# Softmax sums applied to the gate tile instead of p, and hi and lo of p accumulated in the same columns

## The chip, the core and the metric

The kernel runs on one core of a Trainium2 chip. The metric is device microseconds for one execution of the whole program, as a median of runs. Engines are named as in the profile: PE is TensorE's matmul, PEld its weight load, DVE is VectorE, ACT ScalarE, POOL GpSimd, and SP the engine that issues all the DMAs here.

## What is computed

One inference step of a streaming encoder layer, for 2048 new frames of one stream ("prompt") and 64 frames of a running one ("sample"), in float32:

```
h = h + W_out( concat[ attnA(xn) * silu(gA), hgrn2(xn) * silu(gB) ] ),  xn = RMSNorm(h)
...
s = jnp.einsum('bnqhd,bnkhd->bnhqk', q, k).astype(jnp.float32) * ATTN_SCALE + bias
s = jnp.where(valid[None, :, None], s, NEG_INF)
p = jax.nn.softmax(s, axis=-1).astype(v.dtype)
return jnp.einsum('bnhqk,bnkhd->bnqhd', p, v)
...
o_a = attn_fn(heads(aq), k, v).reshape(B, T, W_A) * jax.nn.silu(ag)
```

Group A is attention with 8 heads of 64: each chunk of 64 frames sees its own chunk and the 8 before it, with a learned bias. Group B is a gated linear recurrence with 4 heads of 128. The change is in group A alone: in the softmax, in p times v, and in the product with the gate silu(gA).

## The kernel before

Frames are taken in four stages (`SUPER`) of 512, 576, 512 and 512, the second of which also holds the 64 sample frames. In each stage TensorE multiplies 32 column blocks of W_in with xn (tiles `acc`), and the attention and the recurrence of the heads whose columns are there run between these multiplications. The last stage is followed by the output projection, also in `acc`. Float32 accuracy comes from splitting operands into a high and a low part (`xh` and `xl`, `w` as a pair, `q` and `ql`, v as [hi | lo] in 128 stationary columns, p as `ph[:, 0]` and `ph[:, 1]`) and adding up the products.

The order of instructions on every engine is fixed when the program is built. Generators describe the pieces of work; a planner (`Plan`, called `C`) keeps an estimated clock for each engine and lets a generator go on when its next piece looks ready (`yield "A", t` means: when the plan's ScalarE gets to time t). Tokens (`tk`) stand for buffers: `pr` (4 tiles of p), `ph` (2), `pv` (1 PSUM bank), `mixa` (2), `sga` (2, the gate), and so on. `C.mm(n)` charges TensorE 12 + n/2.37 ns for a matmul of n columns. Each engine works through its list in order, and a wait of the instruction at the head holds all behind it. SP's list holds the weight loads (`w<-wd`, L437) and every other transfer.

Attention works by pairs of heads, and in a pair by units of 256 queries and one head: (g0, h) with g0 = 0, 256 and h = 0, 1. There are 64 such units. In each:

- `softmax_rows` (L895), once for each 128 queries: scores in PSUM (`s`), bias added and the row's extreme taken by DVE (L911), then `softmax_exp` (L925): ScalarE's exponential with the row sum accumulated (L928), DVE's reciprocal of the sum (L931), and DVE's scaling of the up to 640 columns of p by it (L932).
- `p_group` transposes p through PSUM (`tr`, L253), and `split_p` writes hi (ScalarE, L940) and lo (DVE, L943) of the transposed p to `ph`.
- `attend` (L986) multiplies with v. One matmul (L1038) takes hi and lo of one key block side by side: a key block that both 128-query blocks see gives 2 x 256 = 512 moving columns; the two that only one sees give 2 x 128 = 256. PSUM tile `pv` is 128 partitions (64 of v's hi, 64 of v's lo) x 2 halves (p's hi, p's lo) x 256 queries.
- `finish_pv` (L975): ScalarE copies p_hi v_lo to `mixa` (L978), DVE adds p_hi v_hi and p_lo v_hi (L982).
- `mix_out` (L1081), for a pair's two heads together: POOL multiplies `mixa` with the gate `sga` (L1084), and SP stores it to DRAM (`mixd`, L1089). The output projection reads it back from there much later.

The sample frames go through `sample_a`, which has its own scores and p times v and uses `softmax_exp`, `finish_pv` and `mix_out`.

Of the kernel before, what the change touches and what calls it, by code (L numbers as in the profile page):

```python
# [8 lines left out]
F32 = mybir.dt.float32  # L9
F32R = mybir.dt.float32r  # L10
U32 = mybir.dt.uint32
AF = mybir.ActivationFunctionType
# [5 lines left out]
P = 128  # L18
D = 1024
KT = D // P  # L20
SEQ = 2048
DEC = 64
# [7 lines left out]
PRB = 4  # L30
VTB = 3
# [152 lines left out]
def hymba_step(  # L184
# [24 lines left out]
    act = nc.scalar  # L209
    dve = nc.vector  # L210
    pool = nc.gpsimd
    pe = nc.tensor
    sp = nc.sync
# [12 lines left out]
    def T(pool_, shape, dt, tag, **kw):  # L226
        uid[0] += 1
        return pool_.tile(list(shape), dt, tag=tag, name=f"{tag}_{uid[0]}", **kw)

    def psum(tag, shape=(P, 512), bufs=1):  # L230
        return T(ps, shape, F32, tag, bufs=bufs)
# [16 lines left out]
    def mm(out, w, x, n, slow=False, **kw):  # L248
        pe.matmul(out, w, x, **kw)  # L249
        C.mm(n, slow)  # L250

    def transpose(out, x, idn):
        pe.transpose(out, x, idn)  # L253
        C.now += 110.0

    tk = {k: Tok(C, n) for k, n in dict(acc=2, s_ps=1, tr=2, pv=1, g=1, pr=PRB, ph=2, sig=2, vT=VTB, mixa=2,
                                     w=WBUFS, raw=RAWB, xn=XNB, kv0=1, kv1=1, rec=1, sga=2, bias0=1, bias1=1, gf=1, gi=1, gg=1,
                                     ck=1, slot=4, x4=0, x5=0).items()}

# [632 lines left out]

        return d, dict(g=ev_g, q=ev_q, k=ev_k, v=ev_v_last if last else ev_v)

    def softmax_rows(d, h, qc, spans, bcol, nk, out):  # L895

        yield lambda: d.q_n[h] >= qc + P and d.k_n[h] >= qc + P and d.bias_at[h] is not None
        yield max(d.q_t[h], d.k_t[h], d.bias_at[h]) + 300.0
        yield from tk["s_ps"].get()
        yield from tk["pr"].get()  # L900
        sps = s_ps()
        for part in (d.q, ql):
            for i, (k0, kn) in enumerate(spans):
                mm(sps[:, i, :kn], part[:, h, qc : qc + P], d.kd[:, h, k0 : k0 + kn], kn,
                   start=part is d.q, stop=part is ql)
        t = C.pe()
        yield "D", t
        s = T(wk, [P, 640], F32, "pr", bufs=PRB)
        nm = T(wk, [P, 2], F32, "nm", bufs=4)
        ns, kn = len(spans), spans[0][1]  # L910
        dve.tensor_tensor_reduce(  # L911
            s[:, :nk].rearrange("p (a c) -> p a c", a=ns), sps[:, :ns, :kn],
            d.bias[:, h, bcol : bcol + nk].rearrange("p (a c) -> p a c", a=ns),
            1.0, 3e38, ALU.add, ALU.min, nm[:, 0:1])
        t = C.dve(nk + 80, t)
        tk["s_ps"].put(1, t)
        d.left[h] -= 1
        if d.left[h] == 0:
            if h and d.sb == len(SUPER) - 1 and d.p == NPAIR - 1:
                have.add("scores")  # L920
                tk["x4"].put()
            tk[f"bias{h}"].put()
        yield "A", t
        yield from softmax_exp(s, nm, nk, out, t)

    def softmax_exp(s, nm, nk, out, t):
        sm = T(wk, [P, 1], F32, "sm", bufs=4)
        act.activation(s[:, :nk], s[:, :nk], AF.Exp, bias=nm[:, 0:1], scale=-1.0, accum_out=sm)  # L928
        t = C.act(nk + 300, t)
        yield "D", t  # L930
        dve.reciprocal(sm, sm)  # L931
        dve.tensor_scalar(s[:, :nk], s[:, :nk], sm, None, ALU.mult)  # L932
        t = C.dve(0.55 * nk + 150, t)
        out.append((s, t))

    def vcols(v, t, h, rows):
        return (v[:rows, h, t] if v is room["v"] else v[:rows, t, 2 * h : 2 * h + 2, :]).rearrange("p s d -> p (s d)")
# [34 lines left out]
        tk["tr"].put(1, t)  # L972
        done.append((ph, t))

    def finish_pv(h, pv, mix, qn, t):  # L975

        hs, ls = own[h], own[1 - h]
        act.copy(mix[hs, :qn], pv[ls, 0, :qn])  # L978
        t = C.act(qn, t)
        yield "D", t  # L980
        for i in range(2):
            dve.tensor_add(mix[hs, :qn], mix[hs, :qn], pv[hs, i, :qn])  # L982
            t = C.dve(qn, t)
        return t

    def attend(d, g0, h, prs, mixes, before, mine):  # L986

        t0 = SUPER[d.sb][0]
        b0 = (t0 + g0) // P
        base = t0 // P - 4  # L990
        yield lambda: len(prs[0]) and len(prs[1])
        yield max(prs[0][0][1], prs[1][0][1]) + 300.0

        def piece(kt, b):
            pr = prs[b][0][0]
            nk = min(5, b0 + b + 1) * P
            first = b0 + b + 1 - nk // P
            return (pr, (kt - first) * P, b * P)

        items = [(kt - base, P, [piece(kt, 0), piece(kt, 1)]) for kt in range(max(0, b0 - 3), b0 + 1)]  # L1000
        if b0 - 4 >= 0:
            items.append((b0 - 4 - base, P, [piece(b0 - 4, 0)]))
        items.append((b0 + 1 - base, P, [piece(b0 + 1, 1)]))
        groups, cur, used = [], [], 0
        for it in items:
            w = P * len(it[2])
            if used + w > 512:
                groups.append(cur)
                cur, used = [], 0
            cur.append((it, used))  # L1010
            used += w
        groups.append(cur)
        dones = [[] for _ in groups]
        yield lambda: before is None or before["spawned"]
        for i, (g, dn) in enumerate(zip(groups, dones)):
            C.spawn(p_group(g, dn, 2 if i == len(groups) - 1 else 0, turn["given"]), 1)
            turn["given"] += 1
        mine["spawned"] = True
        yield lambda: before is None or before["pv"]
        yield from tk["pv"].get()  # L1020
        mine["pv"] = True
        if h == 0:
            yield from tk["mixa"].get()
            mixes[g0] = T(wk, [P, 256], F32, "mixa", bufs=2)
        mix = mixes[g0]
        yield lambda: d.v_n[h] >= g0 + 256
        yield d.v_t[h]
        pv = psum("pv").rearrange("p (s q) -> p s q", s=2)
        k = 0
        for g, dn in zip(groups, dones):  # L1030
            yield lambda: len(dn)
            ph, t = dn[0]
            yield t + 200.0
            for it, off in g:
                t_, kr, qs = it
                w = P * len(qs)
                q0 = qs[0][2]
                mm(pv[:, :, q0 : q0 + w], vcols(d.v, t_, h, kr), ph[:kr, :, off : off + w], 2 * w,  # L1038
                   start=(k == 0), stop=(k == len(items) - 1))
                k += 1  # L1040
            tk["ph"].put(1, C.pe())
        t = C.pe()
        yield "A", t
        t = yield from finish_pv(h, pv, mix, 256, t)
        tk["pv"].put(1, t)
        mine["end"] = True
        if h:
            yield from mix_out(d, mix, g0, 256, t, g0 + 256 == SUPER[d.sb][1])

    last_mark = [None]  # L1050

    def attention(d):

        sb, p = d.sb, d.p
        t0, n = SUPER[sb][:2]
        npr = min(n, WIN)
        units = [(g0, h) for h in range(2) for g0 in range(0, npr, 256)]
        d.left = [len(units) + (1 if npr < n else 0)] * 2
        allprs = []
        for g0, h in units:  # L1060
            prs = [[], []]
            for b in range(2):
                blk = (t0 + g0) // P + b
                nk = min(5, blk + 1) * P
                qc = g0 + b * P
                k0 = 512 + qc + P - nk
                spans = [(k0, 320), (k0 + 320, 320)] if nk == 640 else [(k0, nk)]
                C.spawn(softmax_rows(d, h, qc, spans, 640 - nk, nk, prs[b]), 1)
            allprs.append(prs)
        marks = [dict(spawned=False, pv=False, end=False) for _ in units]  # L1070
        mixes = {}
        for i, ((g0, h), prs) in enumerate(zip(units, allprs)):
            C.spawn(attend(d, g0, h, prs, mixes, marks[i - 1] if i else last_mark[0], marks[i]), 1)
        last_mark[0] = marks[-1]
        if npr < n:
            yield from sample_a(d, npr, marks)
        for h in range(2):
            yield lambda: all(m["end"] for m, u in zip(marks, units) if u[1] <= h)
            tk[f"kv{h}"].put(1, C.pe())

    def mix_out(d, mix, g0, n, t, last):  # L1081
        yield lambda: d.sg_n >= g0 + n
        yield "P", t
        pool.tensor_mul(mix[:, :n], mix[:, :n], d.sg[:, g0 : g0 + n])  # L1084
        t = C.pool(n + 50, t)
        if last:
            tk["sga"].put()
        yield t
        sp.dma_start(mixd[d.sb][d.p, :, g0 : g0 + n], mix[:, :n])  # L1089
        tk["mixa"].put()  # L1090
        done_a[d.sb] = done_a.get(d.sb, 0) + n
# [32 lines left out]
    def sample_a(d, c0, marks):  # L1124
# [74 lines left out]
        t = C.pe()  # L1199
        yield "A", t  # L1200
        for h in range(2):
            t = yield from finish_pv(h, pv[:, h], mix, DEC, t)
        tk["pv"].put(1, t)
        tk["raw"].put(2)
        C.spawn(mix_out(d, mix, c0, DEC, t, True), 1)
# [953 lines left out]
```

## Time and profile before

| what | value |
|---|---|
| median of 3 runs | 1257.12 us (1254.45 to 1257.91) |
| profiled execution | 1256.82 us |
| its span (first to last instruction) | 1254.6 us |
| mean granted TensorE clock | 0.996 of full speed |
| ACT L928, exponentials of the softmax | 132, 100.3 us |
| DVE L943, lo of the transposed p | 176, 101.4 us |
| DMA queue of SP | 67.4% of 16 engines' time, 286.58 MB |

The profile is of one execution. A row of groups reads: line, engine, operation, out<-in, shape, count | busy us, mean ns of one | idle time of the engine just before it, and what ended it. A row of the timeline reads: start, length of the run of like instructions (both in us), engine, line, operation, shape, count. A row of stretches reads: the stretch, its length, the busy time and count of PE, PEld, DVE, ACT, POOL, then the granted TensorE clock, the DMA engines' busy share and GB/s. A row of waits reads: who waited for whom, us in total, times, longest. A row of DMA issues: out<-in, queue, count, KB each, median us from issue to landing.

### The profile page before, as it was taken

How to read it: one execution, taken by the hardware profiler on the slowest of the kernel's cores; microseconds unless marked ns; L12 is line 12 of the kernel's file. 1: busy time of each engine (PE TensorE's matmuls, PEld its weight loads, DVE VectorE, ACT ScalarE, POOL GpSimd, SP SyncE). 2: the span in 40 equal slices, each digit the busy share in tenths (PEclk: the TensorE clock that was granted, in tenths of full speed). 3: DMA queues.
4: the chain of work that ended last, by engine and by line, in shares of the span. 5: the costliest groups of instructions: out<-in, count | busy, mean ns of one | idle time of the engine just before them, and what ended most of it. 6: DMA issues, size and time to landing. Idle time of an engine off the chain costs nothing. (4 is left out here: it accounts for less than half of the span.)

```text
span 1254.6 us, 21417 instructions
## 1 busy us (share of the span) xinstructions
PE 1240.9 (99%) x7550; PEld 1093.7 (87%) x7550; DVE 894.6 (71%) x1887; ACT 684.7 (55%) x1533; POOL 415.2 (33%) x700
## 2 busy tenths in 40 slices
PE   8999999999999999999999999999999999999997
PEld 8888888999999999998888888988888888888786
DVE  6687879766867678687486667785857476867775
ACT  5354546654656556574465556665655445643443
POOL 6666665111120110201233242134241103474543
PEclk9999999999999999999999999999999999999999
DMA  8987779656555476655777878677666665987431
GB/s 334 311 306 248 279 285 370 212 158 228 178 189 159 145 223 216 193 166 172 252 266 240 299 255 281 227 248 251 219 244 202 222 219 197 342 275 241 136 125 67
DMA packets 137956, 287.94 MB, mean 230 GB/s; under 512 B 35257, under 2 KB 79289, under 8 KB 120186
## 3 DMA queue, kind: packets, MB, share of 16 engines
q1 hardware_dynamic: 137560, 286.58, 67.4%
q8 instruction: 59, 0.97, 0.3%
q14 instruction: 47, 0.39, 0.1%
q10 hardware_dynamic: 290, 0.01, 0.0%
HBM read 195.31 MB, written 92.27 MB: 229 GB/s over the span
## 5 line engine op out<-in xcount | busy, mean ns | idle before, releaser
L249 PE MATMUL acc<-xh,w 128*128 128x512 f32 (+2 forms) x2752 | 566.4, 345 | 0.7 <-ACT xh L403 0.4
L249 PEld LDWEIGHTS acc<-xh,w 128*128 128x128 f32 x2752 | 439.8, 189 | 50.4 <-issue 0.6
L249 PE MATMUL acc<-xl,w 128*128 128x512 f32 (+2 forms) x1376 | 293.4, 345 | 0.3 <-DVE xl L407 0.3
L249 PEld LDWEIGHTS acc<-xl,w 128*128 128x128 f32 x1376 | 220.2, 189 | 25.1 <-DVE xl L407 0.5
L928 ACT ACTIVATE pr<-pr,nm 128x640 f32<-128x640 f32 (+4 forms) x132 | 100.3, 760 | 59.7 <-DVE nm L911 58.8
L940 ACT CAST ph<-tr 128x512 fp32r<-128x512 f32 (+3 forms) x176 | 87.9, 507 | 74.1 <-PE pv L249 47.8
L464 POOL TENSOR_TENSOR w<-wraw,w 128x256 fp32r<-128x256 f32 x120 | 106.6, 914 | 56.9 <-DVE w L459 40.4
L943 DVE TENSOR_TENSOR ph<-tr,ph 128x512 fp32r<-128x512 f32 (+3 forms) x176 | 101.4, 588 | 27.6 <-ACT ph L940 26.8
L911 DVE CUSTOM_DVE_ANT_0 pr<-s,bias 128x640 f32<-128x640 f32 (+4 forms) x128 | 94.2, 736 | 34.8 <-PE s L249 34.1
L249 PE MATMUL pv<-ph,v 128*128 128x256 f32 (+2 forms) x344 | 97.8, 370 | 0.0
L253 PE MATMUL tr<-ident,pr 128*128 128x128 f32 x580 | 89.0, 273 | 1.4 <-DVE sig L634 0.6
L500 POOL TENSOR_TENSOR xn<-wraw,xn 128x256 fp32r<-128x256 f32 x48 | 39.4, 822 | 142.2 <-ACT xn L497 136.4
L982 DVE TENSOR_TENSOR mixa<-mixa,pv 64x256 f32<-64x256 f32 (+1 forms) x144 | 56.8, 395 | 36.0 <-ACT mixa L978 32.7
L1084 POOL TENSOR_TENSOR mixa<-mixa,sga 128x256 f32<-128x256 f32 (+1 forms) x36 | 29.1, 808 | 158.8 <-DVE mixa L982 146.3
L932 DVE TENSOR_SCALAR pr<-pr,sm 128x640 f32<-128x640 f32 (+4 forms) x132 | 76.9, 583 | 4.7
L253 PEld LDWEIGHTS tr<-ident,pr 128*128 128x128 f32 x580 | 69.9, 140 | 10.8 <-DVE sig L634 1.0
L1521 POOL TENSOR_TENSOR k<-ob 128x512 f32<-128x512 f32 (+2 forms) x20 | 18.2, 911 | 180.7 <-ACT ob L1512 161.9
L564 ACT ACTIVATE sig<-acc 128x512 f32<-128x512 f32 (+2 forms) x64 | 32.0, 499 | 64.8 <-PE acc L249 61.7
L249 PEld LDWEIGHTS pv<-ph,v 128*128 128x128 f32 (+1 forms) x344 | 58.4, 189 | 7.1
L978 ACT COPY mixa<-pv 64x256 f32<-64x256 f32 (+1 forms) x72 | 25.1, 349 | 62.3 <-PE pv L249 58.7
L249 PE MATMUL s<-kd,q 128*128 128x320 f32 (+2 forms) x232 | 56.5, 314 | 0.0
L249 PE MATMUL s<-kd,ql 128*128 128x320 f32 (+2 forms) x232 | 55.7, 310 | 0.0
(324 smaller groups left out, 2140.2 us busy)
## 6 DMA issues: line engine op xcount, KB each, us to landing
w<-wd SPq DMA_DIRECT2D x96, 1024.0 KB, 5.6
wd<-w SPq DMA_DIRECT2D x32, 1024.0 KB, 7.7
wraw<-in_w_in_dram SPq DMA_DIRECT2D x30, 512.0 KB, 5.6
wod<-xn SPq DMA_DIRECT2D x28, 512.0 KB, 5.4
xn<-in_x_prompt_dram SPq DMA_DIRECT2D x23, 512.0 KB, 4.6
bias<-biasd SPq DMA_DIRECT2D x24, 320.0 KB, 5.8
carry<-kd SPq DMA_DIRECT2D x12, 512.0 KB, 3.7
carry<-v SPq DMA_DIRECT2D x12, 512.0 KB, 6.7
```

The lines of the kernel that those rows point to most:

```text
L249: pe.matmul(out, w, x, **kw)
L253: pe.transpose(out, x, idn)
L464: pool.tensor_sub(w[:, 1, k : k + 2], raw[:, k : k + 2], f32(w[:, 0, k : k + 2]))
L500: pool.tensor_sub(f32r(st[:, c.start + 512 : c.stop + 512]), src[:, c], st[:, c])
L564: act.activation(sig[:, :bn], acc, AF.Exp, scale=-1.0)
L911: dve.tensor_tensor_reduce(s[:, :nk].rearrange("p (a c) -> p a c", a=ns), sps[:, :ns, :kn], d.bias[:, h, bcol : bcol + nk].rearrange("p (a ...
L928: act.activation(s[:, :nk], s[:, :nk], AF.Exp, bias=nm[:, 0:1], scale=-1.0, accum_out=sm)
L932: dve.tensor_scalar(s[:, :nk], s[:, :nk], sm, None, ALU.mult)
L940: act.copy(ph[:krows, 0, :wid], pt[:krows, :wid])
L943: dve.tensor_sub(ph[:krows, 1, :wid], pt[:krows, :wid], f32(ph[:krows, 0, :wid]))
L982: dve.tensor_add(mix[hs, :qn], mix[hs, :qn], pv[hs, i, :qn])
L1084: pool.tensor_mul(mix[:, :n], mix[:, :n], d.sg[:, g0 : g0 + n])
```

## The change

Three things are changed in the attention of the prompt frames.

1. p is no longer scaled. `softmax_rows` takes the exponential itself and leaves the two row sums of a unit side by side in a tile `sums`; p goes on unnormalised to the transposes.
2. A new generator `weigh` takes the reciprocals of both sums at once, stores them to DRAM as two rows of 128 (`way`, 4 bytes at a time, since a query is a partition in `sums`), and when both heads of a query pair are there, loads them back into `rr`: head 0's 256 numbers into each of 64 partitions, head 1's into the other 64. `mix_out` multiplies the gate tile with `rr` on POOL, and then `mixa` with the gate as before. `rr` has one buffer, guarded by a token.
3. In `attend` hi and lo of p are two matmuls that accumulate in the same 256 columns of `pv`, instead of one that writes both halves beside each other. `finish_pv` then adds one part fewer. (p_lo v_lo is now part of the result too; before, it was computed and not read.)

The sample frames keep the old scaling and the old halves.

```diff
-    def softmax_rows(d, h, qc, spans, bcol, nk, out):
+    def softmax_rows(d, h, qc, spans, bcol, nk, out, sums):
...
-        yield from softmax_exp(s, nm, nk, out, t)
+        if "t" not in sums:
+            sums["t"] = T(wk, [P, 2], F32, "sums", bufs=3)
+        b = qc // P % 2
+        act.activation(s[:, :nk], s[:, :nk], AF.Exp, bias=nm[:, 0:1], scale=-1.0, accum_out=sums["t"][:, b : b + 1])
+        out.append((s, C.act(nk + 300, t)))
+
+    def weigh(d, g0, h, prs, sums, spread):
+
+        yield lambda: len(prs[0]) and len(prs[1])
+        yield "D", max(prs[0][0][1], prs[1][0][1])
+        dve.reciprocal(sums["t"], sums["t"])
+        yield C.dve(60)
+        uid[0] += 1
+        room = dr.tile([2, P], F32, tag=f"way{uid[0]}", name=f"way{uid[0]}")
+        sp.dma_start(room.rearrange("b q -> q b"), sums["t"])
+        t = C.dma(16)
+        spread[g0, h] = room
+        if h == 0:
+            return
+        yield from tk["rr"].get()
+        rr = spread[g0] = T(wk, [P, 256], F32, "rr", bufs=1)
+        yield t
+        for i in range(2):
+            sp.dma_start(rr[own[i]], spread[g0, i].rearrange("(o b) q -> o (b q)", o=1).broadcast_to([64, 256]))
+        sums["at"] = C.dma(32)
...
-        act.copy(mix[hs, :qn], pv[ls, 0, :qn])
+        act.copy(mix[hs, :qn], parts[0][ls])
...
-        for i in range(2):
-            dve.tensor_add(mix[hs, :qn], mix[hs, :qn], pv[hs, i, :qn])
+        for x in parts:
+            dve.tensor_add(mix[hs, :qn], mix[hs, :qn], x[hs])
...
-        pv = psum("pv").rearrange("p (s q) -> p s q", s=2)
+        pv = psum("pv")[:, :256]
...
-                mm(pv[:, :, q0 : q0 + w], vcols(d.v, t_, h, kr), ph[:kr, :, off : off + w], 2 * w,
-                   start=(k == 0), stop=(k == len(items) - 1))
-                k += 1
+                for part in range(2):
+                    mm(pv[:, q0 : q0 + w], vcols(d.v, t_, h, kr), ph[:kr, part, off : off + w], w,
+                       start=k == 0, stop=k == 2 * len(items) - 1)
+                    k += 1
...
+        if by:
+            yield lambda: "at" in by[1]
+            yield "P", by[1]["at"]
+            rr = by[0][g0]
+            pool.tensor_mul(d.sg[:, g0 : g0 + n], d.sg[:, g0 : g0 + n], rr[:, :n])
+            tk["rr"].put(1, C.pool(n + 50))
         yield "P", t
         pool.tensor_mul(mix[:, :n], mix[:, :n], d.sg[:, g0 : g0 + n])
```

Because the planner decides the order, the change moves instructions on every engine. Three places follow; the number behind an underscore is the buffer's, and lines are those of the kernel the row is from.

TensorE's list at the last unit of the last stage (`pv` is the product of `ph` with v; `acc<-xh,slot` and `acc<-w,slot` are the output projection). Before:

```order
L249 MATMUL pv_13179<-ph_13142,v_589 128x512 x2
L249 MATMUL pv_13179<-ph_13156,v_589 128x512 x2
L249 MATMUL acc_13168<-xh_153,slot_13062 128x512 x2
L249 MATMUL acc_13168<-xl_154,slot_13062 128x512
L249 MATMUL acc_13168<-xh_153,slot_13062 128x512 x2
L249 MATMUL acc_13168<-xl_154,slot_13062 128x512
L249 MATMUL acc_13197<-xh_153,slot_13064 128x512 x2
L249 MATMUL pv_13179<-ph_13185,v_589 128x2x128 x2
```

And now:

```order
L249 MATMUL pv_13403<-ph_13349,v_589 128x256 x4
L249 MATMUL acc_13382<-xl_154,slot_13215 128x512
L249 MATMUL acc_13382<-xh_153,slot_13215 128x512 x2
L249 MATMUL acc_13382<-xl_154,slot_13215 128x512
L249 MATMUL acc_13417<-w_13008,slot_13345 128x512 x2
L249 MATMUL pv_13403<-ph_13380,v_589 128x256 x4
L249 MATMUL acc_13417<-w_13067,slot_13345 128x512
L249 MATMUL acc_13417<-w_13008,slot_13345 128x512 x2
L249 MATMUL acc_13417<-w_13067,slot_13345 128x512
L249 MATMUL acc_13417<-w_13008,slot_13345 128x512 x2
L249 MATMUL pv_13403<-ph_13412,v_589 128x128 x4
```

Each group of two matmuls has become one of four with half the columns, and stands between other matmuls of the projection.

SP's list in the third stage, around a weight load (`w<-wd`) of the third pair of heads (`way<-vT` and `carry` belong to other work). Before:

```order
L502 DMA wod_66_138<-xn_8662 256x1x512
L864 DMA carry_2_26_98<-v_589 128x2x512
L437 DMA w_9391<-wd_39_111 128x2048
L680 DMA way_9400<-vT_9379 32x4x128 x4
L437 DMA w_9461<-wd_43_115 128x2048
L502 DMA wod_70_142<-xn_8661 256x1x512
```

And now:

```order
L938 DMA way_9513<-sums_9455 128x2x1
L864 DMA carry_2_26_98<-v_589 128x2x512
L437 DMA w_9543<-wd_39_111 128x2048
L680 DMA way_9549<-vT_9539 32x4x128 x4
L947 DMA rr_9515<-way_9374 64x256
L947 DMA rr_9515<-way_9513 64x256
L437 DMA w_9620<-wd_43_115 128x2048
```

The store of the reciprocals (L938) stands ahead of one weight load, and the two loads of `rr` (L947) ahead of the next.

POOL's list at the same pair of heads (`mixa` times `sga` is the gate; `k<-ob` and `ob` belong to the recurrence, `xn<-wraw` to the output weights). Before:

```order
L500 TENSOR_TENSOR xn_8661<-wraw_8660,xn_8661 128x256 x2
L1084 TENSOR_TENSOR mixa_9211<-mixa_9211,sga_8881 128x256
L1521 TENSOR_TENSOR k_1880_9725<-ob_9721 128x512
L1084 TENSOR_TENSOR mixa_9422<-mixa_9422,sga_8881 128x256
L1543 TENSOR_TENSOR ob_9721<-ob_9721,gg_9451 128x512
```

And now:

```order
L1113 TENSOR_TENSOR sga_9047<-sga_9047,rr_9515 128x256
L1553 TENSOR_TENSOR k_1898_9865<-ob_9861 128x512
L1116 TENSOR_TENSOR mixa_9363<-mixa_9363,sga_9047 128x256
L1113 TENSOR_TENSOR sga_9047<-sga_9047,rr_9889 128x256
L1116 TENSOR_TENSOR mixa_9675<-mixa_9675,sga_9047 128x256
L1575 TENSOR_TENSOR ob_9861<-ob_9861,gg_9611 128x512
```

Each multiplication with the gate has got one with `rr` ahead of it, which waits for the landing of `rr`; the recurrence's products stand behind it.

More of the change, by code (lines that the diff above doesn't have):

```diff
@@ L254, in transpose @@
         C.now += 110.0
-    tk = {k: Tok(C, n) for k, n in dict(acc=2, s_ps=1, tr=2, pv=1, g=1, pr=PRB, ph=2, sig=2, vT=VTB, mixa=2,
+    tk = {k: Tok(C, n) for k, n in dict(acc=2, s_ps=1, tr=2, pv=1, g=1, pr=PRB, ph=2, sig=2, vT=VTB, mixa=2, rr=1,
                                      w=WBUFS, raw=RAWB, xn=XNB, kv0=1, kv1=1, rec=1, sga=2, bias0=1, bias1=1, gf=1, gi=1, gg=1,
@@ L923, in softmax_rows @@
         yield "A", t
-        yield from softmax_exp(s, nm, nk, out, t)
+        if "t" not in sums:
[21 more added lines that the diff above has]
+        sums["at"] = C.dma(32)
     def softmax_exp(s, nm, nk, out, t):
-        sm = T(wk, [P, 1], F32, "sm", bufs=4)
+        sm = T(wk, [P, 1], F32, "sm", bufs=1)
         act.activation(s[:, :nk], s[:, :nk], AF.Exp, bias=nm[:, 0:1], scale=-1.0, accum_out=sm)
@@ L973, in p_group, with finish_pv, attend @@
         done.append((ph, t))
-    def finish_pv(h, pv, mix, qn, t):
+    def finish_pv(h, parts, mix, qn, t):
         hs, ls = own[h], own[1 - h]
-        act.copy(mix[hs, :qn], pv[ls, 0, :qn])
+        act.copy(mix[hs, :qn], parts[0][ls])
         t = C.act(qn, t)
         yield "D", t
-        for i in range(2):
-            dve.tensor_add(mix[hs, :qn], mix[hs, :qn], pv[hs, i, :qn])
+        for x in parts:
+            dve.tensor_add(mix[hs, :qn], mix[hs, :qn], x[hs])
             t = C.dve(qn, t)
         return t
-    def attend(d, g0, h, prs, mixes, before, mine):
+    def attend(d, g0, h, prs, mixes, sums, spread, before, mine):
         t0 = SUPER[d.sb][0]
@@ L1043, in attend @@
         yield "A", t
-        t = yield from finish_pv(h, pv, mix, 256, t)
+        t = yield from finish_pv(h, [pv], mix, 256, t)
         tk["pv"].put(1, t)
@@ L1047, in attend @@
         if h:
-            yield from mix_out(d, mix, g0, 256, t, g0 + 256 == SUPER[d.sb][1])
+            yield from mix_out(d, mix, g0, 256, t, g0 + 256 == SUPER[d.sb][1], (spread, sums[g0, 1]))
     last_mark = [None]
@@ L1058, in attention @@
         d.left = [len(units) + (1 if npr < n else 0)] * 2
-        allprs = []
+        allprs, sums, spread = [], {}, {}
         for g0, h in units:
@@ L1067, in attention @@
                 spans = [(k0, 320), (k0 + 320, 320)] if nk == 640 else [(k0, nk)]
-                C.spawn(softmax_rows(d, h, qc, spans, 640 - nk, nk, prs[b]), 1)
+                C.spawn(softmax_rows(d, h, qc, spans, 640 - nk, nk, prs[b], sums.setdefault((g0, h), {})), 1)
+            C.spawn(weigh(d, g0, h, prs, sums[g0, h], spread), 1)
             allprs.append(prs)
@@ L1072, in attention @@
         for i, ((g0, h), prs) in enumerate(zip(units, allprs)):
-            C.spawn(attend(d, g0, h, prs, mixes, marks[i - 1] if i else last_mark[0], marks[i]), 1)
+            C.spawn(attend(d, g0, h, prs, mixes, sums, spread, marks[i - 1] if i else last_mark[0], marks[i]), 1)
         last_mark[0] = marks[-1]
@@ L1079, in attention, with mix_out @@
             tk[f"kv{h}"].put(1, C.pe())
-    def mix_out(d, mix, g0, n, t, last):
+    def mix_out(d, mix, g0, n, t, last, by=None):
         yield lambda: d.sg_n >= g0 + n
+        if by:
[4 more added lines that the diff above has]
+            tk["rr"].put(1, C.pool(n + 50))
         yield "P", t
@@ L1201, in sample_a @@
         for h in range(2):
-            t = yield from finish_pv(h, pv[:, h], mix, DEC, t)
+            t = yield from finish_pv(h, [pv[:, h, i] for i in range(2)], mix, DEC, t)
         tk["pv"].put(1, t)
```

## Prediction

> **What bounds the kernel now.** I read the page's first table first, then the stretches, then who makes TensorE wait.
>
> ```profile
> span 1254.6 us, 21417 instructions
> PE 1240.9 (99%) x7550; PEld 1093.7 (87%) x7550; DVE 894.6 (71%) x1887; ACT 684.7 (55%) x1533; POOL 415.2 (33%) x700
> ...
> 0.00:100.00 100.00, 96.70 (x533) 82.75 (x534) 74.12 (x132) 49.05 (x102) 65.14 (x107) 0.98 0.84 303
> 100.00:250.00 150.00, 148.52 (x885) 128.04 (x884) 122.19 (x241) 81.83 (x176) 78.53 (x108) 1.00 0.81 288
> ...
> 400.00:550.00 150.00, 150.00 (x1143) 145.29 (x1142) 110.25 (x288) 90.42 (x224) 19.39 (x67) 1.00 0.61 192
> ...
> 1107.00:1255.00 148.00, 139.59 (x610) 112.88 (x608) 102.78 (x154) 61.20 (x154) 73.83 (x86) 0.98 0.51 162
> ```
>
> TensorE (PE) has 13.7 us without a matmul in 1254.6, and 8.4 of them lie after 1107 us, in the output projection. In the stretch from 400 to 550 us it is busy for all 150.00 us at a granted clock of 1.00, while VectorE (DVE) has 40 us to spare. A matmul's bar includes the pipeline's latency, so 99% does not prove that the array is full; the distance between starts does that, and it is read below. Who is waited for:
>
> ```profile
> PE g L1953 <- POOL one L279: 1.4, 1, 1.4
> ...
> PE tr L253 <- DVE pr L932: 0.5, 1, 0.5
> ...
> PE acc L249 <- DVE slot L1684: 0.3, 1, 0.3
> ```
>
> These are the first, one inner and the last of the 11 rows of TensorE's waits. All 11 sum to 7.0 us, and the normalisation of p at L932, which the change removes, accounts for 0.5 us of them. So the time is the sum of the matmuls' spacings, and an edit counts by what it does to that sum. Other engines' work counts only if TensorE comes to wait for it.
>
> **The matmuls of p times v.** Before, one instruction of line 1038 streams hi and lo of p side by side; now each half is an instruction of its own.
>
> ```profile
> L249 PE MATMUL pv<-ph,v 128*128 128x512 f32 x224 | 73.2, 409 | 0.0
> L249 PE MATMUL pv<-ph,v 128*128 128x256 f32 x112 | 25.3, 295 | 0.0
> L249 PEld LDWEIGHTS pv<-ph,v 128*128 128x128 f32 x336 | 57.0, 189 | 6.6
> ```
>
> 224 matmuls of 512 columns become 448 of 256, and 112 of 256 columns (two stretches of 128) become 224 of 128. Columns stay the same; instructions rise by 336, and each brings its own weight load, as the 336 loads for 336 matmuls show. What a matmul costs in a full stream is the distance from its start to the next one's start:
>
> ```profile
> 320.37 1.09 PE L249 MATMUL pv<-ph,v 128*128 128x512 f32 x4
> 321.31 0.46 PE L249 MATMUL acc<-xl,w 128*128 128x320 f32 x2
> ...
> 324.08 0.40 PE L249 MATMUL pv<-ph,v 128*128 128x256 f32 x2
> 324.32 0.60 PE L253 MATMUL tr<-ident,pr 128*128 128x128 f32 x4
> ...
> 325.93 1.12 PE L249 MATMUL acc<-xl,w 128*128 128x256 f32 x8
> 326.89 0.31 PE L249 MATMUL s<-kd,q 128*128 128x320 f32 x1
> ...
> 607.48 2.00 PE L249 MATMUL acc<-xh,w 128*128 128x512 f32 x8
> 609.32 1.98 PE L249 MATMUL acc<-xl,w 128*128 128x512 f32 x8
> ...
> 311.53 0.38 PE L249 MATMUL g<-asb,gi 128*128 128x128 f32 x2
> 311.75 0.39 PE L249 MATMUL g<-bm,stp 128*128 128x128 f32 x2
> 311.97 0.39 PE L249 MATMUL g<-asb,gi 128*128 128x128 f32 x2
> 312.19 0.39 PE L249 MATMUL g<-bm,S 128*128 128x128 f32 x2
> ```
>
> 512 columns: (321.31 - 320.37)/4 = 0.235 us in p times v, and (609.32 - 607.48)/8 = 0.230 in the projection. 256 columns: 0.24/2 = 0.120, and 0.96/8 = 0.120 again. 128 columns: (312.19 - 311.53)/6 = **0.110 us**. From 512 to 256 the spacing halves; from 256 to 128 it hardly falls. That is the point of the forecast.
>
> The first kind: 224 x (2 x 0.120 - d), with d from 0.230 to 0.235, is 1.1 to 2.2 us; I take **+2 us**, nearer the cleaner run of eight. The second kind: 112 x (2 x 0.110 - 0.120) = **+11.2 us**. The halves keep the same stationary operand, so one may ask whether the second one needs its load. The spinning matmuls at the start answer that: they all use the identity.
>
> ```profile
> L1953 PE MATMUL g<-ident 128*128 128x128 f32 x38 | 7.6, 383 | 1.4 <-POOL one L279 1.4
> L1953 PEld LDWEIGHTS g<-ident 128*128 128x128 f32 x38 | 7.1, 289 | 2.2 <-POOL one L279 1.4 <-issue 0.8
> ...
> 8.48 1.92 PE L1953 MATMUL g<-ident 128*128 128x128 f32 x8
> ...
> 8.70:10.00 1.30, 1.30 (x8) 0.50 1.02 416
> ```
>
> 38 matmuls have 38 loads. Eight of them fill 1.92 us; without the last one's own bar (some 0.42) that is 1.50/7 = 0.214 us each at a granted clock of 0.50, or 0.107 us at full clock, although the weights never change. So a load of 128 columns sets the floor, changed or not, and 0.110 stands.
>
> The Trainium skill says otherwise: "TensorE: Matmul & The Clock Gate", section "Back-to-back issue gap", gives N/2.4 + 2.5 ns for an isolated gap, some 56, 109 and 216 ns at 128, 256 and 512 columns. By that rule both edits together would add 224 x 2.5 + 112 x 2.5 ns, under 1 us, and the kernel would stay where it is. The same page, section "LDWEIGHTS (loading the stationary operand)", gives 128 columns / 1.2 = 107 ns for a load, and that is what the rows at 128 columns follow.
>
> **The softmax side.** It removes DVE work.
>
> ```profile
> L931 DVE RECIPROCAL sm<-sm 128x1 f32<-128x1 f32 x132 | 20.3, 153 | 9.4 <-ACT pr L928 8.4
> L932 DVE TENSOR_SCALAR pr<-pr,sm 128x640 f32<-128x640 f32 (+4 forms) x132 | 76.9, 583 | 4.7
> L982 DVE TENSOR_TENSOR mixa<-mixa,pv 64x256 f32<-64x256 f32 x128 | 53.3, 417 | 29.3 <-ACT mixa L978 26.3 <-DMA xn<-in_x_prompt_dram 0.2
> ```
>
> 128 of the 132 scalings go (75 us), 132 reciprocals become 4 and 64 of two columns (about 10 us less), and half of 128 additions go (27 us): some 111 us of DVE's 894.6. TensorE got none of that time: its waits show 0.5 us for L932. The bounds are 0 and the 7.0 us of all rows; I take **-0.5 us**, the row of the removed instruction. ScalarE keeps its 128 exponentials; only the accumulator's target changes.
>
> **The round trip.** For each of 64 units a store of 1 KB in 256 pieces of 4 bytes, and for each of 32 query pairs two loads that spread 1 KB over 64 partitions, then one more multiplication on GpSimd (POOL). No transfer of 4-byte data is in this trace; the nearest rows:
>
> ```profile
> way<-vT SPq DMA_DIRECT2D x72, 64.0 KB, 4.7
> ...
> ck<-in_cache_attn_k_dram SPq DMA_DIRECT2D x16, 64.0 KB, 3.1
> way<-vT SPq DMA_DIRECT2D x32, 8.0 KB, 2.9
> ...
> L1084 POOL TENSOR_TENSOR mixa<-mixa,sga 128x256 f32<-128x256 f32 x32 | 27.3, 853 | 146.3 <-DVE mixa L982 146.3
> ...
> SPq L437 <- PE acc L249: 255.7, 73, 12.0
> ...
> 1095.91 0.83 ACT L928 ACTIVATE pr<-pr,nm 128x640 f32<-128x640 f32 x1
> ...
> 1111.94 0.73 POOL L1084 TENSOR_TENSOR mixa<-mixa,sga 128x256 f32<-128x256 f32 x1
> ```
>
> A store like the 8 KB one (2.9 us) or the one in short runs (3.1), and a load of 64 KB like the 4.7 row: about 7.8 us, an estimate. From the last exponential to the multiplication it is wanted by, the last unit has 1111.94 - 1096.74 = 15.2 us, so the trip usually fits beside the transposes and p times v. Where it does not, POOL stands in its queue, and behind it are the recurrence's products (L1521, L1543 before) and the output weights' residuals (L500). POOL already stands 146.3 us before its multiplication at L1084 without TensorE waiting for it: after the start no row of TensorE's waits names POOL. The 32 new multiplications (32 x 0.853 = 27 us) go to an engine that is 33% busy. In SP's queue the new loads stand ahead of weight loads (L437), but those now wait 255.7 us, over 73 times, for a buffer that TensorE has not yet freed, so SP is ahead of need. I take **0** for the trip; the bounds are a gain of nothing and a loss priced under the second rival.
>
> **Sum.** Profiled execution: 1254.6 of span and 2.2 around it, 1256.8 us. +2 + 11.2 - 0.5 + 0 = +12.7, so 1269.5 in terms of that execution; the median of the runs, 1257.1, is 0.3 above it. I say **1270 us**, 1.0% slower.
>
> **Rivals.**
> 1. *The short halves cost their columns only* (not slower). The line through 256 and 512 columns, 0.120 and 0.230, gives 0.065 us at 128. Then the second kind adds 112 x (2 x 0.065 - 0.120) = 1.1 us, and the whole comes to 1256.8 + 2 + 1.1 - 0.5 = 1259.4, inside 0.3%. It decides if a second half with unchanged weights starts less than about 0.075 us after the first. Against it: 0.110 in the recurrence and 0.107 with the identity. The Trainium skill's gap rule above is this rival's.
> 2. *The round trip becomes a wait of TensorE.* For it: the DMA engines are busy for 0.84 and 0.81 of the first two stretches above, POOL is busiest there (it splits the input weights), and the second query pair of a head pair may load its reciprocals only when the first has been multiplied (one buffer of them). One landing of 4.7 us shown in each of the first stage's four head pairs adds 19 us: 1289. Against it: the 15 us of room and the idle POOL and SP rows.
> 3. *The freed DVE pays.* If all 7.0 us of TensorE's waits vanished and the first rival held too, 1253. It needs both, and the waits are mostly of the start and the end, where the change does nothing.
>
> **How the numbers follow.** Forecast 0.81, first rival 0.07, second 0.10, third 0.02. About 0.3%, 3.8 us, is what a measurement of this kernel can tell from no change. Slower by more than that: forecast and second rival, 0.90 after leaving 0.01 of the forecast's low end to "same"; same 0.08; faster 0.02. The forecast's own bounds: all of the waits gained, 1256.8 + 1.1 + 11.2 - 7.0 = 1262, and above it part of the round trip shown. The range 1261 to 1282 leaves out the first and third rival (0.09) and the far part of the second (about 0.08).
>
> **What would show it.** In the profile after: p times v as 448 matmuls of 256 columns 0.120 us apart and 224 of 128 columns 0.110 apart; 7886 matmuls and as many loads; weight loads busy some 63 us more (336 x 0.189); DVE near 784 us, POOL near 442; TensorE's waits still under 10 us in all and no row of POOL or DMA among them. Wrong would be a spacing near 0.065 at 128 columns (first rival), or waits of TensorE on POOL, `rr` or a late weight (second).

## The result and the profile after

The changed kernel takes **1452.8 us** (median of 4 runs, 1444.3 to 1460.6) against 1257.5: a ratio of 1.155, interval 1.149 to 1.160. The sign was forecast, the size was not: 15.5% slower, where 1.0% was expected. The profiled execution has this page (second line: busy time per engine):

```profile
span 1449.2 us, 22142 instructions
PE 1310.9 (90%) x7886; PEld 1156.4 (80%) x7886; DVE 798.3 (55%) x1631; ACT 684.5 (47%) x1533; POOL 434.5 (30%) x732
...
q1 hardware_dynamic: 160088, 290.84, 77.5%
...
PE 44%; DMA 34%; DVE 6%; ACT 5%; issue 4%; SPq 3%; POOL 3%; POOLq 0%; DVEq 0%; ACTq 0%
```

The 7886 matmuls are those of the forecast. Weight loads are busy 62.7 us longer, which meets the forecast's 63 by luck: in `pv_only` below, with as many loads and the clock of before, it is 23.6 us, and the rest here goes with longer loads at a lower clock (a load for `xh` 196 ns in the mean, 189 before). The span grew by 194.6 us. TensorE without a matmul grew from 13.7 to 138.3 us (+124.6), its busy time by 70.0. The last line is the chain that ended last, by engine: 34% of the span is DMA. The queue row says why that is odd: 1.5% more bytes (290.84 MB for 286.58), yet its packets took 77.5% of a span that is itself 15.5% longer. In engine time that is 0.775 x 1449.2 = 1123 us for 0.674 x 1254.6 = 846.

The stretches (columns as before the change):

```profile
100.00:250.00 150.00, 128.25 (x634) 105.98 (x634) 82.24 (x156) 59.43 (x124) 73.82 (x119) 0.91 0.89 244
400.00:550.00 150.00, 137.95 (x998) 133.97 (x996) 79.55 (x218) 71.89 (x178) 22.94 (x70) 0.94 0.68 165
...
485.00:495.00 10.00, 5.88 (x26) 5.89 (x27) 6.22 (x17) 7.24 (x20) 1.04 (x5) 0.66 0.82 31
```

From 100 to 250 us the DMA engines are busier than before (0.89 for 0.81) and move less (244 GB/s for 288). In the ten microseconds of the third row they are 82% busy with 31 GB/s: busy, but not moving data. TensorE lacks work there for 4 us and its granted clock is down to 0.66. Rows of p times v, from the timeline (start, length, ...), show both speeds:

```profile
418.07 1.11 PE L249 MATMUL pv<-ph,v 128*128 128x256 f32 x8
419.02 0.62 PE L253 MATMUL tr<-ident,pr 128*128 128x128 f32 x4
...
476.75 0.64 PE L249 MATMUL pv<-ph,v 128*128 128x128 f32 x4
477.23 0.51 PE L249 MATMUL acc<-xl,w 128*128 128x320 f32 x2
...
491.74 1.91 PE L249 MATMUL pv<-ph,v 128*128 128x256 f32 x8
493.44 1.47 PE L249 MATMUL acc<-xh,w 128*128 128x320 f32 x6
```

At 418 us eight matmuls of 256 columns take 0.95 us to the next start, 0.119 each, and at 477 us four of 128 take 0.48, 0.120 each: as forecast. At 492 us the eight take 1.70, or 0.213 each: TensorE had stood for 5.7 us until 489.1 (waiting for scores), and its granted clock from 491.7 to 493.5 is 0.50. So idle time is paid twice, once as itself and once as slower matmuls behind it; the mean clock fell from 0.996 to 0.953.

Who is waited for, first by TensorE, then by POOL and by SP:

```profile
PE pv L249 <- DVE v L652: 26.6, 7, 8.4
PE s L249 <- DVE nm L911: 19.6, 4, 5.7
PE tr L253 <- DVE ph L967: 18.9, 6, 5.5
PE g L249 <- ACT k L1495: 14.6, 3, 10.8
...
POOL sga L1113 <- DMA rr<-way: 166.4, 21, 22.1
...
SPq L947 <- DMA way<-sums: 145.2, 20, 15.4
SPq L437 <- PE acc L249: 109.5, 36, 8.2
```

TensorE's rows sum to 131.4 us in 23 rows (7.0 in 11 before). None of them names DMA, and POOL only once, at the start. The first names `v`, which this change does not touch at all. The chain of waits behind the longest of those (8.4 us, ending at 172.4; columns: start, length, what) shows where `v` came from:

```profile
146.87 0.33 DVE pr L911
...
150.02 11.03 DMA way<-vT
161.05 0.02 issue
...
161.14 10.31 DMA vT<-way
...
171.53 0.41 ACT v L649
171.94 0.02 issue
171.97 0.44 DVE v L652
172.40 0.04 issue
172.45 1.11 PE pv L249 x4
```

`v` is turned by a trip through DRAM of its own (also called `way`, L680 and L684). Its store and load took 11.03 and 10.31 us there. In the chain that ended last, transfers of this kind (`way<-vT` and `vT<-way`) stand for 9% and 10% of the whole span. Issues by time to landing, of the changed kernel:

```profile
w<-wd SPq DMA_DIRECT2D x96, 1024.0 KB, 10.5
...
carry<-v SPq DMA_DIRECT2D x12, 512.0 KB, 15.3
...
way<-vT SPq DMA_DIRECT2D x72, 64.0 KB, 10.2
...
rr<-way SPq DMA_DIRECT2D x64, 64.0 KB, 10.2
...
vT<-way SPq DMA_DIRECT2D x20, 128.0 KB, 5.1
...
way<-sums SPq DMA_DIRECT2D x64, 1.0 KB, 10.6
```

and of the kernel before:

```profile
w<-wd SPq DMA_DIRECT2D x96, 1024.0 KB, 5.6
...
carry<-v SPq DMA_DIRECT2D x12, 512.0 KB, 6.7
...
vT<-way SPq DMA_DIRECT2D x20, 128.0 KB, 2.4
```

Several transfers that the change left alone take about twice as long (`w<-wd` 5.6 to 10.5, `way<-vT` 4.7 to 10.2, `carry<-v` 6.7 to 15.3). Not all do: `wraw<-in_w_in_dram` stays at 5.6 and 5.7, and `wod<-xn` lands sooner (5.4 to 3.0). The new store of 1 KB takes 10.6.

### The profile page after: what moved, and what is told of

Read it like the earlier page. It is cut to its first block, busy times and chain, and to the rows that moved or that the text cites. A ratio compares the mean times of both kernels' runs of the same rounds, so it can differ in the third digit from the quotient of the medians.

```text
span 1449.2 us, 22142 instructions
## 1 busy us (share of the span) xinstructions
PE 1310.9 (90%) x7886; PEld 1156.4 (80%) x7886; DVE 798.3 (55%) x1631; ACT 684.5 (47%) x1533; POOL 434.5 (30%) x732
## 3 DMA queue, kind: packets, MB, share of 16 engines
q1 hardware_dynamic: 160088, 290.84, 77.5%
## 4 chain that ended last, share of the span: by engine, by line
PE 44%; DMA 34%; DVE 6%; ACT 5%; issue 4%; SPq 3%; POOL 3%; POOLq 0%; DVEq 0%; ACTq 0%
PE acc L249 30%; DMA vT<-way 10%; DMA way<-vT 9%; PE g L249 5%; DMA w<-wd 4%; PE pv L249 3%; PE tr L253 3%; PE s L249 2%; DMA way<-sums 2%; DMA wod<-xn 2%; SPq L680 2%; DMA wraw<-in_w_in_dram 1%; DMA wraw<-in_w_out_dram 1%; DMA w<-wod 1%; DMA v<-carry 1%
## 5 line engine op out<-in xcount | busy, mean ns | idle before, releaser
L249 PE MATMUL acc<-xh,w 128*128 128x512 f32 (+2 forms) x2752 | 590.5, 355 | 12.9 <-DVE gg L569 4.3
L249 PEld LDWEIGHTS acc<-xh,w 128*128 128x128 f32 x2752 | 452.1, 196 | 63.3 <-DVE gg L569 5.0
L249 PE MATMUL acc<-xl,w 128*128 128x512 f32 (+2 forms) x1376 | 300.7, 350 | 0.3 <-DVE xl L407 0.3
L249 PE MATMUL pv<-ph,v 128*128 128x256 f32 (+1 forms) x680 | 118.5, 300 | 43.7 <-DVE v L652 26.6
L249 PEld LDWEIGHTS pv<-ph,v 128*128 128x128 f32 x680 | 103.2, 204 | 54.8 <-DVE v L652 28.7
L253 PE MATMUL tr<-ident,pr 128*128 128x128 f32 x580 | 93.0, 282 | 19.5 <-DVE ph L967 18.9
L253 PEld LDWEIGHTS tr<-ident,pr 128*128 128x128 f32 x580 | 70.5, 144 | 28.0 <-DVE ph L967 15.2
L1113 POOL TENSOR_TENSOR sga<-sga,rr 128x256 f32<-128x256 f32 x32 | 24.5, 765 | 193.9 <-DMA rr<-way 166.4
L1006 DVE TENSOR_TENSOR mixa<-mixa,pv 64x256 f32<-64x256 f32 (+1 forms) x80 | 30.1, 376 | 63.1 <-ACT mixa L1002 62.1
L249 PEld LDWEIGHTS s<-kd,q 128*128 128x128 f32 x232 | 40.8, 192 | 26.5 <-DVE nm L911 21.0
L1300 ACT COPY gi<-vT 128x512 f32<-128x512 f32 (+2 forms) x24 | 11.7, 495 | 103.1 <-DMA vT<-way 103.1
L652 DVE TENSOR_TENSOR v<-vT,v 128x128 fp32r<-128x128 f32 (+2 forms) x44 | 15.0, 343 | 81.7 <-ACT v L649 81.4
## 6 DMA issues: line engine op xcount, KB each, us to landing
w<-wd SPq DMA_DIRECT2D x96, 1024.0 KB, 10.5
carry<-v SPq DMA_DIRECT2D x12, 512.0 KB, 15.3
```

Of the source, the lines that this page charges most:

```text
L1006: dve.tensor_add(mix[hs, :qn], mix[hs, :qn], x[hs])
L1113: pool.tensor_mul(d.sg[:, g0 : g0 + n], d.sg[:, g0 : g0 + n], rr[:, :n])
```

## The experiments

Three theories stood at the start. **A**: the stores in 4-byte pieces slow all DMA. **B**: the new waits for the round trip, in SP's and POOL's lists, hold up what stands behind them. **C**: the loads that spread 1 KB over 64 partitions do it. Medians are in us; the last column is the time of SP's queue in the profiled execution (share x span), less that of the kernel before (846 us).

| kernel | median | ratio to before, 95% interval | queue, us more |
|---|---|---|---|
| the change | 1452.8 | 1.1548 (1.1493 to 1.1603) | 278 |
| `pv_only` | 1268.6 | 1.0084 (1.0060 to 1.0109) | 1 |
| `round_only` | 1510.4 | 1.1983 (1.1927 to 1.2038) | 270 |
| `dummy_stores` | 1476.0 | 1.1738 (1.1705 to 1.1770) | 294 |
| `dummy_loads` | 1259.8 | 1.0018 (1.0003 to 1.0033) | 22 |
| `long_runs` | 1275.7 | 1.0133 (1.0108 to 1.0158) | 21 |
| `runs_old_pv` | 1258.7 | 1.0013 (0.9999 to 1.0027) | 11 |
| `dummy_pairs` | 1296.5 | 1.0308 (1.0281 to 1.0336) | 94 |
| `dummy_spaced` | 1258.1 | 1.0003 (0.9990 to 1.0016) | 12 |
| `dummy_64` | 1259.5 | 1.0017 (1.0000 to 1.0034) | 12 |
| `dummy_own` | 1276.2 | 1.0148 (1.0115 to 1.0181) | 78 |
| `pairs` | 1304.8 | 1.0376 (1.0342 to 1.0410) | 117 |

The kernel before had 1257.3 beside the first four experiments, 1257.9 beside `long_runs`, `runs_old_pv`, `dummy_pairs` and `dummy_spaced`, and 1257.3 beside the last three.

### The two halves of the change

`pv_only` is the kernel before with part 3 of the diff and nothing else: L1038 as two matmuls, one addition fewer in `finish_pv`.

> The kernel before with part 3 alone: hi and lo of p as two matmuls into the same columns, one addition less; p is scaled as before, no round trip. If the matmul spacings were right (0.120 us at 256 columns, 0.110 at 128), this is 1257 + 13 = 1270 us (1265 to 1275), TensorE waits under 10 us. If the split matmuls are themselves a cause of the 195 us (waits on hi and lo apart, order of TensorE's list), well above 1300.

`round_only` is the change with part 3 taken back.

> The change without part 3: row sums through DRAM to the gate tile, p times v as before. Theory: all of the loss but 13 us comes with the round trip, so 1440 us (1410 to 1460), TensorE waits of over 100 us behind v, scores and transposed p, and a mean granted clock near 0.95. Rival (the split matmuls): near 1257.

p times v in `pv_only`, by shape (count | busy, mean ns | idle before), and its weight loads:

```profile
L249 PE MATMUL pv<-ph,v 128*128 128x256 f32 x448 | 73.5, 288 | 0.0
L249 PE MATMUL pv<-ph,v 128*128 128x128 f32 x224 | 33.6, 266 | 0.0
L249 PEld LDWEIGHTS pv<-ph,v 128*128 128x128 f32 x672 | 93.0, 189 | 4.6 <-DVE mixa L982 0.2
```

No idle time before either shape, a load for each of the 672 matmuls, and +11.2 us in the median: the split of the matmuls is what it was forecast to be. The round trip alone costs more than the whole change (+253 for +195), and more than was expected of it (1410 to 1460 us). So all of the surprise is in the softmax part. Why the unsplit matmuls fare worse with it was not pursued.

### Stores and loads that nobody waits for

`dummy_stores` is the kernel before, with one store per unit of a constant into a DRAM tile that nobody reads, in the form of the change's store. TensorE's order is that of before.

```diff
+        if qc // P % 2:
+            uid[0] += 1
+            room_ = dr.tile([2, P], F32, tag=f"aside{uid[0]}", name=f"aside{uid[0]}")
+            sp.dma_start(room_.rearrange("b q -> q b"), f32(ones)[:, 0:2])
+            C.dma(16)
```

> The kernel before plus 64 stores of a constant tile's 128 x 2 numbers to DRAM in pieces of 4 bytes, where the sums are ready; nothing reads them, nobody waits for them, p is still scaled. Theory A, the small pieces hold up the DMA engines and so all other transfers: most of the loss is here too, 1340 to 1430 us, with way<-vT and w<-wd landing near 10 us instead of 5. Theory B, SP's list stands still while the spreading loads wait for their stores: 1257 to 1265 us here, since no load waits.

`dummy_loads` has the spreading loads alone, 64 of them, into a tile that nobody reads.

```diff
+            rr_ = T(wk, [P, 256], F32, "rr", bufs=1)
+            sp.dma_start(rr_[own[h]], room["aside"].rearrange("(o b) q -> o (b q)", o=1).broadcast_to([64, 256]))
```

> The kernel before plus 64 loads that spread 1 KB of DRAM over 64 partitions into a tile that nobody reads; the 1 KB is written once at the start. Theories A and B: 1257 to 1265 us. Theory C, 64 reads of the same 1 KB hold up the DMA engines: over 1300 us, with packets slow for some microseconds behind each such load.

The page of `dummy_stores`, and two of the rows of TensorE's waits:

```profile
span 1479.4 us, 21503 instructions
...
q1 hardware_dynamic: 154968, 286.64, 77.0%
...
PE pv L249 <- DVE v L652: 33.6, 4, 18.3
PE pv L249 <- DVE ph L948: 19.0, 6, 8.5
```

64 KB of stores (286.58 to 286.64 MB), with no wait and no consumer, cost 218.7 us, more than the whole change and more than A expected (1340 to 1430 us). TensorE's waits name `v` first here too. This trace has no landing times, but SP's wait for the transfers that turn `v` (L684, for `way<-vT`) grew from 34.7 to 127.7 us in all. The loads cost 2.5 us in the median. C falls, and B is not needed. A has its price: 64 x 256 = 16384 pieces bring 294 x 16 / 16384 = 0.29 us of one DMA engine each, counted with what they do to other packets.

The packet records of the two traces say where this time lies, and it is not in the pieces. A packet of 4 bytes takes 9 ns in the median, with the change's kind of store and without. Of the 294 us, 279 lie in packets of over 128 bytes, which belong to other transfers, and there only in the slowest: packets that took over 1 us were 537 before (42 us of 16 engines' time) and are 2156 with the stores (326 us, the longest 10 us), while all the faster ones together stay the same (788 and 782 us). So not every transfer becomes slower; some packets of other transfers are held for microseconds.

### The whole change without the short pieces

`long_runs` keeps the change and its order of waits (load after store, multiplication after load). DVE turns the reciprocals of a query pair by a 32 x 32 transpose in the free `rr`, so that the stores have runs of 128 bytes: four stores for a query pair, once both heads are there, in place of one for each unit.

```diff
+        for i in range(2):
+            dve.reciprocal(rr[:, 32 + 2 * i : 34 + 2 * i], spread[g0, i]["t"])
+        dve.transpose(rr[:, 0:32], rr[:, 32:64])
...
-        sp.dma_start(room.rearrange("b q -> q b"), sums["t"])
+        for a in range(4):
+            sp.dma_start(room[:, 32 * a : 32 * a + 32], rr[32 * a : 32 * a + 4, 0:32])
```

> The whole change, but the reciprocals of both heads are turned by a 32 x 32 transpose on DVE (in the free rr tile) and go to DRAM in 16 runs of 128 bytes for a query pair instead of 512 pieces of 4 bytes; the order of waits (load after store, multiplication after load) stays. Theory A (small pieces hold up the DMA engines): 1266 to 1275 us, the cost of the split matmuls alone. Theory B (standing waits for the round trip in SP's or POOL's list): above 1300 still.

`runs_old_pv` is the same with part 3 taken back.

> As long_runs, with p times v as before the change (hi and lo side by side in one matmul). Theory A: 1252 to 1259 us; freeing about 85 us of DVE gives TensorE at most its 7 us of waits. Theory B: above 1285.

`long_runs`: the queue, the largest of TensorE's waits, POOL's wait for `rr`, and SP's waits on the trip (in this kernel L947 is the store and L950 the load):

```profile
q1 hardware_dynamic: 143704, 290.84, 67.8%
...
PE acc L249 <- ACT vT L762: 2.5, 1, 2.5
...
POOL sga L1116 <- DMA rr<-way: 82.5, 13, 13.0
...
SPq L947 <- DVE rr L942: 64.5, 21, 10.8
...
SPq L950 <- DMA way<-rr: 8.3, 10, 2.7
```

The same 290.84 MB now cost 17.8 us over before in place of 195 (the median is just above the expected 1266 to 1275). SP still stands 64.5 us before the store, for DVE's transpose, and POOL 82.5 us for `rr`, and most of the loss is gone. But the wait of the load for its store fell too, from 145.2 to 8.3 us, so this run alone would not rule B out. `dummy_stores`, which has none of these waits and loses 218.7 us, does so as the main cause. `runs_old_pv`, a round trip of this kind with the old p times v, equals the kernel before (+0.8 us). So a softmax part with runs of 128 bytes costs nothing, and gains nothing either: DVE is freed of 61.6 us there (833.0 for 894.6 busy) and the time does not move. `long_runs` stands 6.6 us further from before than `pv_only` does (17.8 and 11.2); TensorE's waits of 11.9 us for 7.0 are part of it, and the rest was not separated.

### What it is about the pieces

`dummy_pairs` stores both columns of a partition as one piece of 8 bytes (tile [P, 2]), 128 pieces per store. `dummy_spaced` keeps 256 pieces of 4 bytes but puts them 512 bytes apart:

```diff
-            room_ = dr.tile([2, P], F32, tag=f"aside{uid[0]}", name=f"aside{uid[0]}")
-            sp.dma_start(room_.rearrange("b q -> q b"), f32(ones)[:, 0:2])
+            room_ = dr.tile([2, P, 128], F32, tag=f"aside{uid[0]}", name=f"aside{uid[0]}")
+            sp.dma_start(room_[:, :, 0].rearrange("b q -> q b"), f32(ones)[:, 0:2])
```

> dummy_stores with the two numbers of a partition beside each other in DRAM: 128 pieces of 8 bytes instead of 256 of 4, the same bytes. If a piece costs, whatever its size: half of dummy_stores' loss, 1350 to 1390 us. If pieces of 8 bytes do not cost: near 1260. If bytes or stores cost: 1476 as there.

> dummy_stores with each 4-byte piece 512 bytes from the next in DRAM. If pieces hold each other up because they are written into the same stretch of DRAM: near 1260 to 1300 us. If every small piece costs by itself: 1476 as dummy_stores.

Queue and store of `dummy_spaced`:

```profile
q1 hardware_dynamic: 154968, 286.64, 68.3%
...
aside<-ones SPq DMA_DIRECT2D x64, 1.0 KB, 5.1
```

and of `dummy_pairs`:

```profile
q1 hardware_dynamic: 146776, 286.64, 72.7%
...
aside<-ones SPq DMA_DIRECT2D x64, 1.0 KB, 8.3
```

`dummy_spaced` moves the same 154968 packets and 286.64 MB as `dummy_stores`, and its time is that of before. So neither the number of pieces nor their size costs this by itself: it is that they lie **side by side**. Half as many pieces of 8 bytes, side by side, cost 38.6 us, which is none of the three times expected of `dummy_pairs`: less than half of the loss, and more than nothing.

Two more kernels ask how near is too near. `dummy_64` has the pieces 64 bytes apart (tile [2, P, 16]). `dummy_own` has them side by side within each group of 8 partitions, but each group in a row of 512 bytes of its own; it needs two stores per unit, which fill 32 bytes of every row each.

```diff
+            room_ = dr.tile([16, P], F32, tag=f"aside{uid[0]}", name=f"aside{uid[0]}")
+            for b_ in range(2):
+                sp.dma_start(room_[:, 8 * b_ : 8 * b_ + 8], f32(ones)[:, b_ : b_ + 1])
```

> The kernel before with 64 unread stores of 256 pieces of 4 bytes, now 64 bytes apart in DRAM (dense they cost 218 us, 512 bytes apart nothing). If pieces disturb each other only inside one block of 64 bytes or less: 1257 to 1262 us. If blocks up to 512 bytes count: between, 1290 to 1450, a dose that falls with the distance.

> The kernel before with the same 16384 unread pieces of 4 bytes, side by side within each group of 8 partitions (32 bytes), but every group of 8 has a 512-byte row of its own. If it is pieces of different partition groups that disturb each other in a shared row: 1257 to 1265 us. If writes that follow each other within one group and one 64-byte block are enough: 1400 or more.

64 bytes of distance suffice (+2.2 us, at the edge of the noise). `dummy_own` met neither expectation: +18.9 us. Some 200 of the 219 us are therefore gone when a row of 128 neighbours is cut into rows of 8, each of one group of partitions. That it is the meeting of *different* groups that costs, and not the length of the row, is an argument and not shown. The last 19 come from pieces of one group or from the doubled number of stores, which this run does not tell apart. Blocks of 64 bytes would fit the order of the four results: dense 4-byte pieces put two groups into each, `dummy_pairs` and `dummy_own` one, `dummy_64` a single piece. They do not explain the sizes: in queue time a piece costs 94 x 16 / 8192 = 0.18 us in `dummy_pairs` and 78 x 16 / 16384 = 0.08 in `dummy_own`, with one group to a block in both. No run shows such a block as such, and other sizes of group were not tried.

The Trainium skill, "DMA: Bandwidth & Descriptors", section "Specifications", says that below 512 B the DMA does a read-modify-write, and that by convention an engine serves 8 partitions. The second is consistent with `dummy_own`, though no run here shows which engine took which piece. The first alone would price `dummy_spaced` like `dummy_stores`; the runs say 1258.1 and 1476.0.

### The price in the change itself

`pairs` is the change with the store's pieces of 8 bytes; order and waits are the change's.

```diff
-        room = dr.tile([2, P], F32, tag=f"way{uid[0]}", name=f"way{uid[0]}")
-        sp.dma_start(room.rearrange("b q -> q b"), sums["t"])
+        room = dr.tile([P, 2], F32, tag=f"way{uid[0]}", name=f"way{uid[0]}")
+        sp.dma_start(room, sums["t"])
...
-            pool.tensor_mul(d.sg[:, g0 : g0 + n], d.sg[:, g0 : g0 + n], rr[:, :n])
+            sg_ = d.sg[:, g0 : g0 + n].rearrange("p (b q) -> p b q", b=2)
+            pool.tensor_mul(sg_, sg_, rr[:, :n].rearrange("p (q b) -> p b q", b=2))
```

> The whole change, but each unit's reciprocals are stored as 128 pieces of 8 bytes (both sums of a query next to each other) in place of 256 pieces of 4; the load brings them back in that order and POOL reads them with a stride of two. Order of all instructions as in the change. If the price hangs on the short pieces lying side by side, as the two kernels with unread stores said (174 to 218 us with pieces of 4 bytes, 38 us with half as many of 8): p times v +11, pieces +30 to +45, so 1298 to 1320 us. If the waits for the round trip in SP's and POOL's lists are most of it: still about 1450.

```profile
way<-sums SPq DMA_DIRECT2D x64, 1.0 KB, 6.2
```

1304.8 us, inside the forecast of theory A. TensorE's matmuls run in the order of the change, and an edit of where the bytes lie in DRAM, which also halves the number of pieces, takes 148 us off the change. TensorE's waits fall from 131.4 to 26.4 us, and the store lands in 6.2 us for 10.6. None of the kernels is faster than the one before.

## Why the prediction was wrong

- **p times v, +13.2 us: right.** `pv_only` measures +11.2 (both edits together). First rival, that short halves cost only their columns (1259.4, +2.6), is refuted. By the gap rule of the Trainium skill, "TensorE: Matmul & The Clock Gate", section "Back-to-back issue gap", which gives it for an isolated matmul, the split would have added under 1 us; the trace shows 0.120 us each for four matmuls of 128 columns (476.75 to 477.23 above) and 0.119 each for eight of 256. The forecast of 63 us more of weight loads was too high: it priced 336 new loads at the row's mean of 189 ns, but loads overlap, and `pv_only` adds 36.0 us in p times v (93.0 for 57.0) and 23.6 in all.
- **The freed DVE, -0.5 us: right in kind.** DVE fell to 798.3 us (784 forecast) and `runs_old_pv` shows that this gains nothing. Third rival refuted.
- **The round trip, 0: this is the step that failed.** It took the store as "like the 8 KB one (2.9 us) or the one in short runs (3.1)". Those transfers come in pieces of 128 bytes, and no data in the trace came in pieces of 4, so the landing time of the nearest row said nothing of what the pieces do to other transfers, and no upper bound of that kind was kept. The runs put some 177 us on the 4-byte pieces in the change (195 less the 17.8 of `long_runs`) and 219 on the bare stores.
- **"SP is ahead of need": true, at most, of weight loads.** L437's wait for TensorE did shrink (255.7 to 109.5 us) without being used up. But the transfers that turn `v` and the recurrence's tiles were not covered by that row, and with landings of 10 us TensorE came to wait for `v`.
- **The 15.2 us of room: too little.** Store and load now land in 10.6 and 10.2 us, 20.8 together, so POOL waits 166.4 us for `rr`. In `long_runs`, with the same consumer, POOL still waits 82.5 us, and the whole change is within 18 us of before; in `dummy_stores` nobody waits for a trip, and the loss is there. So this wait is a symptom and not the main cost.
- **Second rival, that the trip becomes a wait of TensorE: right in direction, wrong in mechanism and size.** It priced one landing per head pair, 19 us, through POOL and `rr`. The loss came through transfers that the change left alone, ten times as large.
- **What would show it.** "TensorE's waits still under 10 us in all" failed with 131.4. "No row of POOL or DMA among them" held, but for POOL at the start, and would have misled: the rows name the last link (DVE, ACT), and the chain behind the longest of them leads to DMA.

The 194.6 us of the two profiled spans, from the page's rows: 124.6 of TensorE idle; 70.0 of longer busy time, of which the split explains 11.3 (1252.2 in `pv_only` for 1240.9) and the rest goes with the lower clock after the idle stretches.

## What to carry to other kernels

Price a transfer not only by when it lands but by what it does to the others on the same engines: if the trace of before has no transfer with pieces of that size *and* that layout, leave the upper end open, or try the bare transfer, with nobody waiting for it, in the old kernel. To lay a column of partitions out along DRAM, turn it on chip first (`runs_old_pv`) or keep the pieces apart (shown for the store alone; the load back from spaced pieces was not tried). And when TensorE's waits name an operand that the change does not touch, follow its chain to the first transfer and compare landing times row by row.

## What the runs showed of the hardware

- Stores of 4-byte pieces side by side in DRAM hold up other transfers: 16384 of them, 64 KB, add 294 us of 16 engines' time and 219 us to the kernel. The pieces' own packets take 9 ns each in the median; the time is in packets of other transfers that take over 1 us, 2156 for 537 before. 64 or 512 bytes apart, the same pieces add 12 us of queue time, and 2.2 and 0.2 us to the kernel.
- The profile counts an engine with a held-up packet as busy: 0.82 busy at 31 GB/s. High DMA share with low GB/s was the sign.
- Behind 5.7 us in which TensorE stood for lack of operands, its granted clock was 0.50, and matmuls of 256 columns went from 0.119 to 0.213 us apart.
